# First block of an encoder step: next token rows loaded whole, cached forget logits and constants loaded earlier, query pieces in key tiles

## The chip, the core and the metric

The kernel runs on one core of one Trainium2 chip. The engines of the core work side by side, each through its own queue in order: TensorE (PE; weight loads are shown as PEld), VectorE (DVE), ScalarE (ACT), GpSimd (POOL) and SyncE (SP), which issues most DMAs. An instruction that waits holds up all that stand behind it in its queue. The metric is device time in microseconds; less is better.

## The reference

One inference step of one encoder layer for 2048 prompt tokens and 64 sample tokens with 512 cached positions. Everything is float32.

```python
h = rmsnorm(x, g_pre)
proj = jnp.einsum('bsd,dc->bsc', h, w_in)            # 1024 -> 4104 columns
fq, fk, fv, ff, fg, dq, dk, dv, dg = jnp.split(proj, SPLIT_POINTS, axis=-1)
logf = log_sigmoid(ff + b_f)
cum = jnp.cumsum(logf_all, axis=1)                   # sample: behind the cached logits
fox_o = fox_attention(fq, fk_all, fv_all, cum, ...)  # 8 heads of 64, decay by cum[t] - cum[s]
lam = exp(sum(lq1 * lk1)) - exp(sum(lq2 * lk2)) + lam_init
diff_o = diff_attention(dq1, dq2, dk1, dk2, dv, lam, rel_bias, ...)   # 4 heads
diff_o = rmsnorm(diff_o, subln_g) * (1.0 - lam_init)
mixed = concatenate([fox_o * silu(fg), diff_o * silu(dg)])
y = x + rmsnorm(einsum('bsc,cd->bsd', mixed, w_out), g_post)
```

Returned are y for both token sets and the new rows of fk, fv, logf, dk and dv.

## The kernel before

Each float32 operand of a large product is split into a high and a low part, and a product is three matmuls: high by high, low by high, high by low (L871, L872, L873; for query groups L1026 to L1028). The prompt is cut into four blocks of 512 tokens; the first block carries the 64 sample tokens too. Per block the kernel does the projection in eight column groups of 512: `fv`, `fg`, `fk`, `fq`, `dg`, `dk`, `dq`, `dv`, numbered `gi` 0 to 7 (values, gate, keys and queries of the forgetting attention, `f`, and gate, keys, queries, values of the differential one, `d`). Attention and output projection of earlier blocks run beside the projection of later ones; in the first block there is only the projection, until its attention begins.

A weight group comes in eight row tiles of 128. Each is loaded into a staging tile `wst` (L773; two of them share one buffer of pool `p`, eight buffers), cast on ACT to the high part `wh` (L776), and its rest is made on DVE or POOL as the low part `wl` (L777). The normalised input is kept transposed: `xraw` is loaded (L740), scaled and cast on ACT (`xx`, L744), and DVE makes its low half (L745; L748 for the sample tokens).

The factor 1/rms of each token is applied when a product leaves PSUM (L881 on ACT, into a tile `ef` of four buffers). For the first block the sums of squares come from PE (`ptq`, L1118) and `xv` (L1123, DVE) and end in a root refined by L155 to L158. For the second block they come from the token rows themselves: `stats` loads rows of `xp` as tiles `xn` (L1072) and ACT squares and sums them (L1084). The projection of block 0 emits these squares between the tiles of its groups.

The `wst` loads and their casts run ahead of PE: while PE works on one group, the loads of the next two are issued. In the first block the PSUM tiles of products rotate over five buffers (`acc`); besides, three buffers named `pt` serve `ptq`, the sums of the forget gates and the first tiles of the second group. Values leave through `vhl` (stored to `VS`), gates through `gw` (stored to `GS`), keys are transposed on PE (`ptk`) into `khl` (stored to `KS`), queries are scaled into `qf`, split into `qhl` and stored to `QD`, `QN`. `vhl`, `khl` and some `qhl` share a ring of two buffers, `er`. Attention later loads keys `kg`, queries `qg` and values `vg` from there.

`forget` makes the forget gates; in its step `sample` it loads the cached forget logits (`crev`, L1212), scans them in a row (L1216) and stores the sums (`csum`, L1221). `prologue2` loads the small constants: `subl` (a gain of the differential output), `lamt` (the four lambda vectors, broadcast to all partitions, in an `ef` tile), `relT` and `cbias` (the position bias table and one column of it), and computes `neglam` (two sums on DVE, L1418, an exponential on ACT, L1421) and `cbias` negated (L1428).

All these steps are thunks in one long list, `line`, each with an estimated time; the list is sorted by it and run, and a scheduler then orders the instructions of each engine. `prologue2` has the time 110.0.

## Time and profile before

| what | us |
|---|---|
| runs, median (lowest to highest) | 1772.97 (1772.33 to 1780.28) |
| the profiled execution | 1778.38 |
| its span in the trace | 1776.6 |
| PE busy in the span | 1715.1 |
| DVE, ACT, POOL busy | 1208.8, 1127.0, 761.7 |

The profile gives, for one execution, the busy time of each engine, what ended each idle time, and when each DMA was issued and landed. A row of a timeline reads: start, duration, engine, line and operation, tile written and read, shape, and in brackets the idle time before it and what ended that. `SPq` is SP's queue of DMA issues. PEclk is the clock that PE was granted, 1.00 being full speed.

### The profile page before, as it was taken

How to read it: one execution, taken by the hardware profiler on the slowest of the kernel's cores; microseconds unless marked ns; L12 is line 12 of the kernel's file. 1: busy time of each engine (PE TensorE's matmuls, PEld its weight loads, DVE VectorE, ACT ScalarE, POOL GpSimd, SP SyncE). 2: the span in 40 equal slices, each digit the busy share in tenths (PEclk: the TensorE clock that was granted, in tenths of full speed). 3: DMA queues.
4: the chain of work that ended last, by engine and by line, in shares of the span. 5: the costliest groups of instructions: out<-in, count | busy, mean ns of one | idle time of the engine just before them, and what ended most of it. 6: DMA issues, size and time to landing. Idle time of an engine off the chain costs nothing.

```text
span 1776.6 us, 31312 instructions
## 1 busy us (share of the span) xinstructions
PE 1715.1 (97%) x9844; PEld 1462.7 (82%) x9844; DVE 1208.8 (68%) x3289; ACT 1127.0 (63%) x2518; POOL 761.7 (43%) x1075
## 2 busy tenths in 40 slices
PE   8899999999999999999999999999989999999998
PEld 6697988888787877888888888888878888888887
DVE  5424565566786666766777687877788787767674
ACT  5636465586676765675676567667676656666663
POOL 2313135364444533443324235645685655323341
PEclk9899999999999999999999999999999999999999
DMA  9785688889767667877677666767674455355433
GB/s 249 229 218 185 201 279 284 242 268 278 210 224 242 209 184 222 260 206 243 213 249 212 208 178 196 225 201 224 204 235 155 158 184 180 129 204 166 155 109 111
DMA packets 278981, 369.94 MB, mean 208 GB/s; under 512 B 32080, under 2 KB 167404, under 8 KB 278816
## 3 DMA queue, kind: packets, MB, share of 16 engines
q1 hardware_dynamic: 278000, 365.57, 67.0%
q0 software_dynamic: 672, 2.38, 0.5%
q8 instruction: 78, 1.28, 0.3%
q14 instruction: 87, 0.71, 0.1%
q10 hardware_dynamic: 144, 0.00, 0.0%
HBM read 263.87 MB, written 106.35 MB: 208 GB/s over the span
## 4 chain that ended last, share of the span: by engine, by line
PE 71%; DMA 11%; DVE 6%; ACT 4%; issue 3%; POOL 3%; SPq 1%; DVEq 0%; POOLq 0%; ACTq 0%
PE S L348 11%; PE pt L487 8%; PE acc L871 8%; PE acc L872 7%; PE acc L873 7%; PE av L518 6%; PE avd L518 4%; PE acc L1026 3%; PE acc L1027 3%; PE acc L1028 3%; DMA wraw<-in_w_in 3%; PE acco L1325 2%; PE acco L1327 2%; PE acco L1326 2%; ACT prob L369 2%
## 5 line engine op out<-in xcount | busy, mean ns | idle before, releaser
L369 ACT ACTIVATE prob<-prob,mn 128x1024 f32<-128x1024 f32 (+8 forms) x400 | 356.6, 893 | 152.8 <-DVE mn L356 151.6
L348 PE MATMUL S<-kg,qg 128*128 128x512 f32 (+4 forms) x1344 | 370.7, 371 | 10.9 <-DVE mn L356 6.1
L494 DVE TENSOR_TENSOR ptl<-pt,pth 128x512 fp32r<-128x512 f32 (+3 forms) x456 | 283.6, 637 | 80.1 <-ACT pth L493 77.7
L871 PE MATMUL acc<-wh,xx 128*128 128x512 f32 x752 | 300.6, 403 | 14.3 <-DVE xv L1123 6.2
L872 PE MATMUL acc<-wl,xx 128*128 128x512 f32 x752 | 299.5, 400 | 3.9 <-DVE wl L777 3.9
L873 PE MATMUL acc<-wh,xx 128*128 128x512 f32 x752 | 298.6, 398 | 0.3 <-DVE xx L745 0.2
L493 ACT CAST pth<-pt 128x512 fp32r<-128x512 f32 (+3 forms) x456 | 238.1, 546 | 91.1 <-PE pt L487 78.4
L487 PE MATMUL pt<-ident,prob 128*128 128x128 f32 (+2 forms) x1692 | 256.4, 273 | 7.7 <-DVE prob L596 5.2
L348 PEld LDWEIGHTS S<-kg,qg 128*128 128x128 f32 (+1 forms) x1344 | 225.5, 187 | 46.4 <-DVE mn L356 11.5
L487 PEld LDWEIGHTS pt<-ident,prob 128*128 128x128 f32 (+2 forms) x1692 | 199.3, 141 | 28.1 <-DVE prob L596 6.1
L777 POOL TENSOR_TENSOR wl<-wraw,wh 128x512 fp32r<-128x512 f32 x126 | 169.7, 1363 | 90.9 <-ACT wh L776 85.0
L871 PEld LDWEIGHTS acc<-wh,xx 128*128 128x128 f32 x752 | 143.4, 191 | 43.8 <-issue 6.6
L872 PEld LDWEIGHTS acc<-wl,xx 128*128 128x128 f32 x752 | 143.4, 191 | 30.0 <-DVE wl L777 4.6
L873 PEld LDWEIGHTS acc<-wh,xx 128*128 128x128 f32 x752 | 143.0, 190 | 28.6 <-DVE xx L745 1.2
L518 PE MATMUL av<-pth,vg 128*128 128x256 f32 (+1 forms) x576 | 157.5, 292 | 3.9 <-ACT pth L493 2.3
L405 POOL TENSOR_TENSOR dg<-bias,cmask 128x128 f32<-128x128 f32 (+1 forms) x136 | 65.2, 479 | 208.6 <-DVE mn L356 134.0
L450 POOL TENSOR_SCALAR gate<-gate,rr 128x64 f32<-128x64 f32 (+1 forms) x136 | 64.2, 482 | 182.8 <-DMA gate<-GS 98.9
L518 PE MATMUL av<-ptl,vg 128*64 128x256 f32 (+1 forms) x576 | 138.2, 281 | 1.5 <-DVE ptl L494 1.5
L776 ACT CAST wh<-wraw 128x512 fp32r<-128x512 f32 x168 | 100.6, 621 | 58.3 <-DMA wraw<-in_w_in 44.1
L518 PE MATMUL avd<-pth,vg 128*128 128x256 f32 (+1 forms) x576 | 131.4, 287 | 0.4 <-ACT pth L493 0.4
L356 DVE CUSTOM_DVE_ANT_0 prob<-S,bias,mn 128x512 f32<-128x512 f32 (+4 forms) x200 | 115.4, 577 | 13.6 <-PE S L348 6.6
L518 PEld LDWEIGHTS av<-pth,vg 128*128 128x128 f32 x576 | 109.5, 191 | 14.2 <-ACT pth L493 2.7
(261 smaller groups left out, 3604.6 us busy)
## 6 DMA issues: line engine op xcount, KB each, us to landing
wraw<-in_w_in SPq DMA_DIRECT2D x168, 256.0 KB, 5.2
vg<-VS SPq DMA_DIRECT2D x80, 512.0 KB, 6.3
qg<-QD SPq DMA_DIRECT2D x128, 256.0 KB, 4.4
kg<-KS SPq DMA_DIRECT2D x64, 512.0 KB, 5.1
wst<-in_w_in SPq DMA_DIRECT2D x64, 256.0 KB, 6.3
out<-ef SPq DMA_DIRECT2D x64, 256.0 KB, 2.6
VS<-vhl SPq DMA_DIRECT2D x32, 512.0 KB, 4.8
KS<-khl SPq DMA_DIRECT2D x32, 512.0 KB, 4.4
```

The source lines that it names most:

```text
L348: nc.tensor.matmul(S[:rows, :c1 - c0], q()[s][:, qc:qc + rows], kg()[ki][:, c0 - k0:c1 - k0], start=(s == 0), stop=(s == 1))
L356: nc.vector.tensor_tensor_reduce(out=pr[:rows, a - p0:b - p0], in0=S[:rows, a - c0:b - c0], in1=ap()[:rows, a - b0:b - b0], scale=1.0, sca ...
L369: nc.scalar.activation(out=pr, in_=pr, func=AF.Exp, scale=-1.0, bias=st["m"][:rows, i - 1:i], accum_out=st["s"][:rows, h:h + 1])
L487: nc.tensor.transpose(pt[:rk, off:off + rows], self.key_tile(sts[j], rows, kt, rk), ident[:rows, :rows])
L493: nc.scalar.copy(h[:rk, :off], pt[:rk, :off])
L494: nc.vector.tensor_tensor(out=l[:rk, :off], in0=pt[:rk, :off], in1=r32(h[:rk, :off]), op=ALU.subtract)
L518: nc.tensor.matmul(st["av"][:vs.stop - vs.start, j0 * rows:W], ctxu["v"][kt // 4][:rk, kt % 4, vs], g["p"][part][:rk, o:o + w], start=(kt ...
L776: nc.scalar.copy(h, raw[:, :BLK])
L777: (nc.vector if many or k % 4 == 3 else nc.gpsimd).tensor_tensor(out=l, in0=raw[:, :BLK], in1=r32(h), op=ALU.subtract)
L871: nc.tensor.matmul(a, x[0][:, c0:c0 + rows], wh, start=s, stop=False)
L872: nc.tensor.matmul(a, x[0][:, c0:c0 + rows], wl, start=False, stop=False)
L873: nc.tensor.matmul(a, x[1][:, c0:c0 + rows], wh, start=False, stop=e)
```

## The change

Four edits, all in the projection of the first block and in the constants.

1. The token rows for the second block's statistics are loaded whole, 128 by 1024 in four loads from pool `p`, the weights' ring, instead of eight halves from pool `raw`; one load is ahead of its square instead of two, the second half of the sums `xss` is zeroed, and the squares are emitted with groups 4 and 5 instead of 2 to 5.
2. The cached forget logits are loaded where `forget` allocates its first tile, into a tile of pool `b`; the same tile holds `csum`. Scan and negation thus no longer use two `ef` tiles.
3. The four loads of `prologue2` form a function `loads2` of their own with time 60.0; `lamt` gets a tile of pool `g`. The sums over it and all other arithmetic stay in `prologue2` at 110.0 in the list; the scheduler orders them by when their inputs are asked for.
4. Query pieces of group `fq` that went to the ring `er` go to tiles of the keys' pool `k`.

```diff
@@ -839,7 +839,7 @@
                     for tt in ts:
                         last = tt[-1] == tl[-1]
                         th += self.nat(b, g, tt, w, x, cols, st, last and ends, last and lastg)
-                        if 2 <= gi <= 5:
+                        if (2 if b else 4) <= gi <= 5:
                             th += sq[:1]
                             sq = sq[1:]
                         if b == 0 and gi == 1 and tt[0] == tl[2]:
@@ -1037,6 +1037,7 @@
                     def evac(c=c, i=i, e=e, segs=segs, t0=t0, N=N):
                         f = self.p["e"].tile([P, BLK], F32, name="qf", tag="ef")
                         hl = self.p["raw"].tile([P, BLK], F32R, name="qhl", tag="raw") if nt > BLK and not i else \
+                            self.p["k"].tile([P, 2 * BLK], F32R, name="qhl", tag="k") if nt > BLK and g == "fq" else \
                             self.p["e"].tile([P, 2 * BLK], F32R, name="qhl", tag="er", bufs=2)
                         nc.vector.tensor_tensor(out=f[:, :N], in0=e[i][:, :N], in1=st["rbc"][:, t0:t0 + N],
                                                 op=ALU.mult)
@@ -1060,16 +1061,16 @@
             tl = tilesof[b]
             e = {}
 
-            todo = [(i, t, hf) for i, t in enumerate(tl) for hf in (0, 1)]
-            lead = 2 if b == 1 else 1
+            parts, w = (1, D) if b == 1 else (2, BLK)
+            todo = [(i, t, hf) for i, t in enumerate(tl) for hf in range(parts)]
+            lead = 1
 
             def load(n):
                 i, t, hf = todo[n]
-                e[n] = self.p["raw"].tile([P, BLK], F32, name="xn", tag="raw") if b == 1 else \
+                e[n] = self.p["p"].tile([P, 2 * BLK], F32, name="xn", tag="p") if b == 1 else \
                     self.p["e"].tile([P, BLK], F32, name="xn", tag="ef")
-                nc.sync.dma_start(out=e[n], in_=xp[t * P:(t + 1) * P, hf * BLK:(hf + 1) * BLK])
+                nc.sync.dma_start(out=e[n], in_=xp[t * P:(t + 1) * P, hf * w:(hf + 1) * w])
 
             def square(n):
                 def go():
@@ -1077,6 +1078,8 @@
                     if not n:
                         e["ss"] = sm.tile([P, 2, 8], F32, name="xss", tag="xss", bufs=2)
                         nc.vector.memset(e["ss"], 1.0)
+                        if parts == 1:
+                            nc.vector.memset(e["ss"][:, 1, :], 0.0)
                         for m in range(lead):
                             load(m)
                     if n + lead < len(todo):
@@ -1134,6 +1137,10 @@
 
             def alloc():
                 e["z"] = self.p["raw"].tile([P, BLK + DEC], F32, name="z8", tag="z", bufs=1)
+                if b == 0:
+                    t = self.p["b"].tile([P, BW], F32, name="crev", tag="b")
+                    e["rev"], e["csum"] = t[:8, :BLK], t[:8, BLK:]
+                    nc.sync.dma_start(out=e["rev"], in_=clf)
             th.append((0.0, alloc))
             for c0, N in ((0, BLK), (BLK, DEC))[:1 + (b == 0)]:
                 def step(c0=c0, N=N):
@@ -1206,10 +1213,8 @@
                 nc.sync.dma_start(out=lf_s, in_=z[:DEC, 32:40])
                 pt = ps.tile([P, BLK], F32, name="pts", tag="pt", bufs=3)
                 nc.tensor.transpose(pt[:8, :DEC], z[:DEC, 32:40], ident[:DEC, :DEC])
-                c = self.p["e"].tile([P, BLK], F32, name="csum", tag="ef")[:8]
+                c, r = e["csum"], e["rev"]
                 c2 = sm.tile([8, DEC], F32, name="csn", tag="csn", bufs=1)
-                r = self.p["e"].tile([P, BLK], F32, name="crev", tag="ef")[:8]
-                nc.sync.dma_start(out=r, in_=clf)
                 nc.vector.tensor_tensor_scan(out=c2, data0=ones[:8].to_broadcast([8, DEC]), data1=pt[:8, :DEC],
                                              initial=0.0, op0=ALU.mult, op1=ALU.add)
                 nc.sync.dma_start(out=CS[:, PAST:], in_=c2)
@@ -1408,23 +1413,29 @@
         nc.vector.tensor_tensor(out=wf[:, :, 32:40], in0=wv, in1=r32(wf[:, :, 0:8]), op=ALU.subtract)
         nc.sync.dma_start(out=fb, in_=bass.AP(fbias.tensor, fbias.offset, [[0, P], [1, 8]]))
 
+    held = {}
+    def loads2(g):
+        nc.sync.dma_start(out=subl, in_=subln)
+        held["lam"] = g.tile([P, 2, P], F32, name="lamt", tag="g").rearrange("p a c -> p (a c)")
+        nc.sync.dma_start(out=held["lam"], in_=bcast_row(lams, 256))
+        held["rt"] = sm.tile([4, 32], F32, name="relT", tag="relT", bufs=1)
+        nc.sync.dma_start(out=held["rt"], in_=relT)
+        nc.sync.dma_start(out=cbias, in_=bass.AP(relT.tensor, relT.offset + 15, [[0, P], [32, 4]]))
     def prologue2(e):
-        nc.sync.dma_start(out=subl, in_=subln)
-        lam = e.tile([P, BLK], F32, name="lamt", tag="ef")
-        nc.sync.dma_start(out=lam[:, :256], in_=bcast_row(lams, 256))
+        lam, rt = held["lam"], held["rt"]
         ee = sm.tile([P, 4], F32, name="lame", tag="lame", bufs=1)
         for i in (0, 1):
-            nc.vector.tensor_tensor_reduce(out=lam[:, 256:320], in0=lam[:, 128 * i:128 * i + 64],
+            nc.vector.tensor_tensor_reduce(out=lam[:, 128 * i:128 * i + 64], in0=lam[:, 128 * i:128 * i + 64],
                                            in1=lam[:, 128 * i + 64:128 * i + 128], scale=1.0, scalar=0.0,
                                            op0=ALU.mult, op1=ALU.add, accum_out=ee[:, i:i + 1])
         nc.scalar.activation(out=ee[:, 2:4], in_=ee[:, 0:2], func=AF.Exp)
         nc.vector.tensor_tensor(out=neglam, in0=ee[:, 3:4], in1=ee[:, 2:3], op=ALU.subtract)
         nc.vector.tensor_scalar(out=neglam, in0=neglam, scalar1=LAM_INIT, scalar2=None, op0=ALU.subtract)
 
-        rt = sm.tile([4, 32], F32, name="relT", tag="relT", bufs=1)
-        nc.sync.dma_start(out=rt, in_=relT)
-        nc.sync.dma_start(out=cbias, in_=bass.AP(relT.tensor, relT.offset + 15, [[0, P], [32, 4]]))
         nc.vector.tensor_scalar(out=cbias, in0=cbias, scalar1=-1.0, scalar2=None, op0=ALU.mult)
         ln = e.tile([P, BLK], F32, name="line", tag="ef")[:4]
         ln2 = e.tile([P, BLK], F32, name="line2", tag="ef")[:4]
@@ -1472,6 +1483,7 @@
         put(lst, t, t + cost(lst))
         if b == 0:
             line.append((20.0, len(line), lambda: prologue(pe)))
+            line.append((60.0, len(line), lambda: loads2(pools["g"])))
             line.append((110.0, len(line), lambda: prologue2(pe)))
             for h in range(4):
                 line.append((150.0 + 25.0 * h, len(line), lambda h=h: prologue3(h)))
```

The lines of the changed kernel are shifted by up to 12 from the place of each edit on. Where the constants are loaded, SP's queue held before, from the last `xraw` of the first block on (`xn` are the token rows, `subl`, `relT` and `cbias` the constants):

```order
L740 DMA xraw<-in_xT 128x576
L773 DMA wst<-in_w_in 128x512 x8
L1072 DMA xn<-in_xp 128x512 x5
L773 DMA wst<-in_w_in 128x512 x2
L1412 DMA subl<-in_subln 128x1
L1426 DMA relT<-in_relT 4x32
L773 DMA wst<-in_w_in 128x512 x2
L1427 DMA cbias<-in_relT 128x4x1
L773 DMA wst<-in_w_in 128x512 x2
L1072 DMA xn<-in_xp 128x512 x2
L773 DMA wst<-in_w_in 128x512 x2
```

The same place on SP in the changed kernel (`crev` are the cached logits, `CS` the store of their sums):

```order
L740 DMA xraw<-in_xT 128x576
L1143 DMA crev<-in_clf 8x512
L773 DMA wst<-in_w_in 128x512 x8
L1420 DMA subl<-in_subln 128x1
L1422 DMA lamt<-in_lams 128x256
L1424 DMA relT<-in_relT 4x32
L1425 DMA cbias<-in_relT 128x4x1
L773 DMA wst<-in_w_in 128x512 x4
L1226 DMA CS<-crev 8x512
L773 DMA wst<-in_w_in 128x512 x4
```

Seven loads of token rows are gone from here; the load of `crev` stands ahead of the eight weight tiles and the four constants stand right behind them, `lamt` among them. The eight are those of group `fk`, the pieces behind them those of `fq`.

On DVE, from the end of the first group's low halves to the root that the first evacuations need, stood before:

```order
L745 SCALAR_TENSOR_TENSOR xx<-xraw,gcol,xx 128x576
L748 SCALAR_TENSOR_TENSOR xx<-xraw,gcol,xx 128x64
L777 TENSOR_TENSOR wl<-wst,wh 128x512 x4
L1123 TENSOR_SCALAR xv<-ptq 128x4
L1123 TENSOR_SCALAR xv<-ptq 64x1
L155 TENSOR_TENSOR rt_463<-xrs 128x8
L156 TENSOR_TENSOR rt_464<-rt_463,xv 128x8
L1428 TENSOR_SCALAR cbias<-cbias 128x4
L157 TENSOR_SCALAR rt_464<-rt_464 128x8
L158 TENSOR_TENSOR xrs<-xrs,rt_464 128x8
```

and now, up to `xv` (behind which the root follows without a row between; ISA rows are the two sums over `lamt`):

```order
L1221 SCALAR_TENSOR_TENSOR crev<-ones,crev 8x512
L745 SCALAR_TENSOR_TENSOR xx<-xraw,gcol,xx 128x576
L748 SCALAR_TENSOR_TENSOR xx<-xraw,gcol,xx 128x64
L1224 TENSOR_SCALAR crev<-crev 8x511
L777 TENSOR_TENSOR wl<-wst,wh 128x512 x2
L1432 ISA lamt,lame<-lamt 128x64
L1432 ISA lame 128x1
L1432 ISA lamt,lame<-lamt 128x64
L1432 ISA lame 128x1
L1439 TENSOR_SCALAR cbias<-cbias 128x4
L1436 TENSOR_TENSOR neglam<-lame 128x1
L1437 TENSOR_SCALAR neglam<-neglam 128x1
L777 TENSOR_TENSOR wl<-wst,wh 128x512 x2
L1126 TENSOR_SCALAR xv<-ptq 128x4
```

The scan of the cached logits moved ahead of the last low half of the input; `lamt`'s sums, `cbias` and `neglam` moved ahead of the last two low weights and of `xv`. At the scan's old place DVE went from the gates straight to `crev` and then to the eight low weights of group `fk`:

```order
L1000 SCALAR_TENSOR_TENSOR gw<-ef,gw 128x512
L1216 SCALAR_TENSOR_TENSOR crev<-ones,crev 8x512
L1218 MEMSET csum 8x1
L1219 TENSOR_SCALAR csum<-crev 8x511
L777 TENSOR_TENSOR wl<-wst,wh 128x512 x8
```

where now the three rows between are gone. The token rows stand further back on SP, at the key stores (`KS`), with the query stores (`QD`) behind:

```order
L970 DMA out<-ef 128x512
L1073 DMA xn<-in_xp 128x1024
L989 DMA KS<-khl 128x8x128
L1073 DMA xn<-in_xp 128x1024 x3
L773 DMA wst<-in_w_in 128x512 x2
L989 DMA KS<-khl 128x8x128
L970 DMA out<-ef 64x512
L773 DMA wst<-in_w_in 128x512 x3
L1052 DMA QD_94<-qhl 128x256
L1053 DMA QD_94<-qhl 128x512
```

Before, the eight `wst` loads of group `dk` stood here in one piece; now four loads of token rows go ahead of it, it comes in pieces of 2, 3 and 3, and the last three stand among the query stores.

## The prediction

> **What bounds the kernel now.** I read the page first: TensorE (PE) works nearly all the time, so a change that adds no matmul can gain only where PE waits or runs at a lowered clock.
> ```profile
> span 1776.6 us, 31312 instructions
> PE 1715.1 (97%) x9844; PEld 1462.7 (82%) x9844; DVE 1208.8 (68%) x3289; ACT 1127.0 (63%) x2518; POOL 761.7 (43%) x1075
> PE   8899999999999999999999999999989999999998
> ```
> The slices with idle time are the first four of 44 us each, which hold the first block's projection, and the change's new order lies there too: behind about 160 us PE, ACT and VectorE (DVE) meet the same instructions in the same order, and time saved ahead of that point reaches the end whole. So the next view is busy time and granted clock of PE in those stretches, cut at its long waits.
> ```profile
> core 0: us, PE busy (x), PEclk, DMA share, GB/s
> 0.00:39.30 39.30, 36.26 (x170) 1.00 0.90 234
> 39.30:45.40 6.10, 0.00 (x0) 0.89 0.97 319
> 45.40:51.00 5.60, 5.57 (x13) 0.51 0.78 258
> 51.00:76.70 25.70, 25.05 (x114) 1.00 0.69 233
> 76.70:80.50 3.80, 0.00 (x0) 1.00 0.50 167
> 80.50:86.00 5.50, 5.46 (x17) 0.69 0.75 263
> 86.00:129.00 43.00, 43.00 (x262) 1.00 0.91 210
> 129.00:139.00 10.00, 6.79 (x50) 1.00 0.82 258
> 139.00:170.00 31.00, 31.00 (x130) 0.94 0.63 200
> ```
> Three stalls, and behind each PE runs for a while at a lowered clock: 5.60 us at 0.51 hold 5.60 × 0.49 = 2.7 us of lost time, 5.50 at 0.69 hold 1.7, and 31 at 0.94 hold 1.9. PE's waits from 0 to 170 us name who released each:
> ```profile
> PE acc L871 <- DVE xv L1123: 6.2, 1, 6.2
> PE acc L872 <- DVE wl L777: 3.9, 1, 3.9
> PE acc L871 <- ACT wh L776: 3.7, 2, 3.2
> PE ptf L1195 <- DVE fz L1187: 0.6, 1, 0.6
> ```
> Columns: total us, times, longest. All that the change can win is 6.2 + 2.7, 3.9 + 1.7, 3.2 + 1.9 and 0.6: some 20 us of 1778.4, the profiled execution's own time.
>
> **The first stall (39.3 to 45.4 us).** The group that follows the first needs PSUM buffers that `ptq` shares, and L1123 reads `ptq` behind the last low weights (L777) on DVE. Those wait for ScalarE (ACT), which waits for the next token rows:
> ```profile
> 40.24 0.63 ACT L1084 ACTIVATE xn<-xn 128x512 f32<-128x512 f32 x1 [7.72 <-DMA xn<-in_xp]
> 44.47 0.69 DVE L777 TENSOR_TENSOR wl<-wst,wh 128x512 fp32r<-128x512 f32 x1 [2.28 <-ACT wh L776]
> 45.08 0.21 DVE L1123 TENSOR_SCALAR xv<-ptq 128x4 f32<-128x4 f32 x2
> ```
> The change takes the squares and their loads out of this place. But in DVE's queue two sums over `lamt`, the negation of `cbias` and two instructions for `neglam` now stand ahead of the last two low weights, and so ahead of `xv`. What is late next is the landing of these constants. They are issued behind eight weight tiles:
> ```profile
> 23.05 6.72 SPq L773 DMA_DIRECT2D wst<-in_w_in  x8
> SPq L1412 <- DMA wst<-in_w_in: 1.2, 1, 1.2
> 39.54 0.33 SPq L1412 DMA_DIRECT2D subl<-in_subln  x1
> 42.26 6.64 DMA cbias<-in_relT
> 48.92 0.17 DVE L1428 TENSOR_SCALAR cbias<-cbias 128x4 f32<-128x4 f32 x1 [2.75 <-DMA cbias<-in_relT]
> ```
> Before, the load at 39.54 us waited 1.2 us for a weight tile, the last of those eight (it is the eighth DMA ahead of `subl`): so these weights have landed only by about 39.5 us, 10 us behind their issue. `cbias` is 2 KB and yet took 6.64 us. If the constants keep their place behind the weights, `cbias` is there between 41 us (39.5 and a short transfer) and 45 us (39.5 + most of 6.64). Behind it DVE still does 0.17 for `cbias`, 0.24 + 0.15 for `neglam`, two low weights at 0.69 and `xv` at 0.21, about 2.2 us. PE starts again between 43.2 and 47.2 us, against 45.4: a gain of 2.2 to a loss of 1.8, and the half clock stays. The value nearest the row is the middle: **0**.
>
> The Trainium skill, page "DMA: Bandwidth & Descriptors", section "Queues, rings and completion order", says that each DMA engine consumes the descriptors of a queue in ring order. That speaks against this edit, since a small load cannot pass 2 MB queued ahead of it; the 6.64 us for 2 KB agree. By the rule this term is 0 or a loss, without it a gain of up to the 8.9 us of the stall and its clock.
>
> **The wait for `fz` (0.6 us).** In the row above, DVE stood 2.75 us for `cbias` in the middle of the root that all evacuations of the first group need. In the new order nothing stands there, so the forget gates come earlier against PE: **+0.6**.
>
> **The second stall (76.7 to 80.5 us).**
> ```profile
> 78.22 1.21 DVE L1216 TENSOR_TENSOR_SCAN crev<-ones,crev 8x512 f32<-8x512 f32 x1 [7.13 <-DMA crev<-in_clf]
> 79.81 4.89 DVE L777 TENSOR_TENSOR wl<-wst,wh 128x512 fp32r<-128x512 f32 x8
> 78.85 0.69 ACT L881 ACTIVATE ef<-acc,xrs 128x512 f32<-128x512 f32 x1 [5.08 <-DMA GS<-ef]
> ```
> DVE waits 7.13 us for the cached forget logits, then scans them, and only then makes the low weights that PE waits for. Loaded ahead of the eight weights at 23.05 us, and scanned there, they are out of DVE's queue here: the low weights follow their casts at once. ACT's wait is another: an evacuation needs an `ef` buffer that a gate store still reads. The two `ef` buffers of the scan are now free, so that evacuation waits for an older store. What I expect is that the stall and its clock go: **+3.9 + 1.7 = 5.6**; should ACT's wait hold the last five casts behind it as now, all but 1 us of it stays (rival C).
>
> The scan itself moves ahead of the last low half of the input:
> ```profile
> 29.01 0.82 DVE L745 SCALAR_TENSOR_TENSOR xx<-xraw,gcol,xx 128x576 fp32r<-128x576 f32 x1 [0.66 <-ACT xx L744]
> 30.50 0.39 PE L871 MATMUL acc<-wh,xx 128*128 128x512 f32 x1
> ```
> With 1.21 us it ends that half near 31.0 instead of 29.8, about when PE wants it. Up to 1 us of delay there lies in front of the first stall, whose end is set by the constants: **0**, and 1 us if that cover is gone.
>
> **The third stall (129 to 139 us).**
> ```profile
> 124.42 0.55 ACT L1049 CAST qhl<-qf 128x256 fp32r<-128x256 f32 x2 [7.55 <-DMA KS<-khl]
> 131.86 1.61 SPq L1415 DMA_DIRECT2D lamt<-in_lams  x1
> 136.28 0.22 DVE L1418 CUSTOM_DVE_ANT_0 lamt<-lamt 128x64 f32<-128x64 f32 x1 [6.91 <-DMA lamt<-in_lams]
> 136.81 0.20 ACT L1421 ACTIVATE lame<-lame 128x2 f32<-128x2 f32 x1 [7.90 <-DVE lame L1418]
> 137.71 0.61 ACT L776 CAST wh<-wst 128x512 fp32r<-128x512 f32 x1
> L348 PE MATMUL S<-kg,qg x54: 220/332/477, 188.4 to 297.3; 128*128 128x128 f32 x14, 128*128 128x256 f32 x14, 128*128 128x384 f32 x14, 128*128 128x512 f32 x12
> ```
> The load of `lamt` is late because it needs an `ef` buffer; DVE and ACT stand 7 to 8 us for it, and the casts that PE waits for stand behind. Both go with the early load; and query pieces that waited 7.55 us for key stores (the shared `er` ring) get `k` buffers. The first key loads of the attention, which owned these, now stand behind the last query stores on SP; the scores (L348, the last row) first read keys at 188.4 us, some 40 us on, which hides it. **+3.2 + 1.9 = 5.1**.
>
> **The moved token rows.** They are 2 MB, as before, now in four loads among the key stores, ahead of the weights of the differential keys, whose last tiles wait until squares have freed the ring; PE asks for those only after the whole gate group, so that they have time.
> ```profile
> 29.82 6.69 SPq L1072 DMA_DIRECT2D xn<-in_xp  x5
> xn<-in_xp SPq DMA_DIRECT2D x7, 256.0 KB, 8.2
> ```
> Before, a 256 KB load landed in 8.2 us; a 512 KB one takes from 8 to 16. On ACT each square is twice 0.63 us at most, four are 5.0. Behind them ACT holds the fox query casts, which PE needs only when its PSUM is full: the first block has five buffers, and a tile of 24 matmuls lasts 24 × 43.00/262 = 3.9 us by the stretch from 86 to 129 us, which gives some 16 us of cover. So **0**, with up to 5 us lost if a load lands later than that cover.
>
> **Sum.** 0 + 0.6 + 5.6 + 0 + 5.1 + 0 = 11.3 us at full price. In no row is the second wait of ACT shown to vanish; I leave 1 us of it. 10.3 us off the profiled 1778.4 make 1768.1; the profiled execution stood 5.4 us above the runs' median of 1772.97, so against the median it is **1762.7 us**.
>
> **Rivals.**
> *A, the forecast*: 0.50; own range 1760 to 1766 (the first term from +2.2 to −1.8, the remainder of the second stall 0 to 2).
> *B, the constants land early.* If the small loads are not held behind the weights, `xv` comes with the last weight at about 40 us; 3 us or less of the first stall is left, and some or all of the 2.7 us of clock goes too: another 3 to 6 us, 1757 to 1760. For it: PE's wait is named to DVE and ACT, not to a DMA. Against: 6.64 us for 2 KB. 0.17. How much of the clock returns, the rows leave open: waits of 3.9 and 3.2 us cost 1.7 and 1.9 us behind them. The Trainium skill, page "TensorE: Matmul & The Clock Gate", section "Part 1: The HAM clock gate (the "warmup" mystery)", has the clock halved after an idle window of about 3.4 us; by that a rest of 3 us would mostly cost none, by the rows in proportion 1.5.
> *C, the second stall stays in part.* ACT's evacuation of the gate group still waits for a gate store that queues behind other transfers: at most 1 of its 5.08 us goes, DVE's low weights then wait for ACT, and PE waits 3 instead of 3.9 us with its clock lowered. The sum is 0.6 + 1 + 5.1, about 6: 1767. 0.20.
> *D, the moved squares keep the third stall.* If a token row lands late, ACT stands at its square, the query casts come behind, and behind these the casts of the gate group, for which PE stopped at 138 us. A delay of 3 us keeps that stall with its clock, 5 us of what is won: 1768 to 1770. 0.08.
> *E, slower.* The moved token rows fill the PSUM cover: squares stand on ACT behind loads that land over 16 us after the first square's turn, query casts stand behind them, and PE stops. It decides from four loads taking more than 16 us together; at a landing of 16 us each, one behind the other from the third on, PE loses 14 us and its clock 2 more, against 11 won: 1778, up to 1784. Nothing in the stretch from 86 to 129 us (DMA 0.91 busy, 210 GB/s) excludes it; that 2 MB at 210 GB/s are 10 us speaks against. 0.05.
>
> **From cases to numbers.** The range 1757 to 1770 holds A, C, nearly all of D and the greater part of B. Half a percent (8.9 us, about what a measurement of this kernel can tell from no change) puts the border of faster at 1764.1, inside A: two thirds of A and all of B give 0.33 + 0.17, a little of C 0.03, faster 0.53; the rest of A, C, D and part of E make 0.44 the same; the upper part of E slower, 0.03.
>
> **What would show it.** PE's first stall ends with `xv` behind `cbias` on DVE, at 43 to 47 us, at half clock after it: A; at 41 us, B. In PE's waits no wait over 1 us for L777 near 77 us, and none for L776 near 138 us; ACT's wait for a gate store under 2 us: otherwise C. No wait of PE for `acc` PSUM near 110 to 125 us: otherwise D or E. The prediction is wrong if DVE stands longer than to 45 us for a constant, or if the gain ahead of 160 us is lost again behind it, where I assume the same order means the same pace.

## The result and the profile after

In 20 runs each, the changed kernel has a median of 1765.95 us (1760.43 to 1773.49) against 1776.81 us (1772.33 to 1783.70) before: a ratio of 0.9938, 95% interval 0.9928 to 0.9949, or 11 us of gain with 9 to 13 as its interval. The prediction had 10.3 us. Its 1762.7 us was counted from the median of three runs before, 1772.97 us, which 20 runs put at 1776.81; so the gain agrees and the time itself lies 3.2 us above. The profiled execution of the changed kernel took 1771.98 us, 6 us above its median, so the spans of the two profiles differ by only 6.4 us.

From the page of the changed kernel, the span, the engines' busy times and PE's slices; then PE's busy time and granted clock, cut at its waits, and the waits themselves from 30 to 200 us:

```profile
span 1770.2 us, 31297 instructions
PE 1712.9 (97%) x9844; PEld 1458.2 (82%) x9844; DVE 1203.0 (68%) x3290; ACT 1125.3 (64%) x2510; POOL 762.7 (43%) x1075
PE   8999999999999999999999999999989999999998
```

```profile
core 0: us, PE busy (x), PEclk, DMA share, GB/s
0.00:41.90 41.90, 37.92 (x170) 0.96 0.89 230
41.90:44.10 2.20, 0.05 (x2) 1.00 0.97 344
44.10:50.00 5.90, 5.85 (x19) 0.71 0.83 281
50.00:69.00 19.00, 19.00 (x90) 1.00 0.76 261
69.00:75.00 6.00, 6.00 (x28) 1.00 0.66 168
...
151.80:155.00 3.20, 0.01 (x1) 1.00 0.41 159
155.00:170.00 15.00, 14.94 (x58) 0.89 0.12 41
```

```profile
PE acc L871 <- ACT wh L776: 3.3, 1, 3.3
PE acc L871 <- DVE xv L1126: 2.2, 1, 2.2
PE ptq L1121 <- POOL xsq L755: 0.7, 1, 0.7
```

The second stall and the third are gone with their lowered clock; the matmuls that stood behind them now start without a wait, at 73.5 and 126.2 us. The first is shorter, and a **new one of 3.2 us** stands at 151.8 us, where the kernel before had none.

To see what each stretch brought, the same matmul is looked up in both traces: both programs have 9844, and the n-th starts earlier in the changed kernel by its *lead*. I take it at four places, named by the time that the kernel before needs: behind the first stall (58.9 us), the second (96.4), the third (147.8) and at 211.6 us, from where PE, ACT and DVE have the same order. One execution has a lead at each place; the first two rows, two executions of the same program, show how much that varies. Each ratio is to runs of the kernel before that were made beside it.

| run | 58.9 | 96.4 | 147.8 | 211.6 | median us | ratio to before (95%) |
|---|---|---|---|---|---|---|
| the change | 2.3 | 8.8 | 14.1 | 7.8 | 1765.95 | 0.9938 (0.9928 to 0.9949) |
| the change, again | 6.4 | 12.6 | 17.9 | 14.0 | 1767.42 | 0.9931 (0.9910 to 0.9953) |
| rows back | 0.3 | 6.8 | 12.1 | 9.9 | 1765.49 | 0.9935 (0.9911 to 0.9959) |
| logits back | 3.2 | 9.7 | 15.0 | 12.4 | 1763.31 | 0.9922 (0.9902 to 0.9941) |
| constants back | 5.5 | 12.0 | 15.6 | 13.3 | 1763.29 | 0.9921 (0.9902 to 0.9941) |
| er ring back | 2.5 | 9.1 | 14.3 | 14.1 | 1763.78 | 0.9920 (0.9901 to 0.9940) |
| er ring, late arithmetic | 7.2 | 8.5 | 13.7 | 13.4 | 1764.15 | 0.9916 (0.9893 to 0.9939) |
| rows alone | 3.9 | 6.7 | 11.9 | 11.9 | 1764.07 | 0.9914 (0.9894 to 0.9934) |
| logits alone | 0.8 | 7.3 | 4.7 | 3.8 | 1775.43 | 0.9977 (0.9963 to 0.9991) |
| constants alone | 0.0 | 2.5 | 7.8 | 3.1 | 1770.03 | 0.9953 (0.9937 to 0.9969) |
| key tiles alone | 0.3 | 0.4 | 3.5 | 1.6 | 1778.28 | 0.9992 (0.9981 to 1.0004) |
| rows and logits | 5.0 | 11.6 | 16.8 | 15.8 | 1762.42 | 0.9905 (0.9885 to 0.9925) |

Behind 212 us the leads of single profiles still drift with the order unchanged: at the end, 1550 us later, they stand between 6.6 us lower and 8.4 us higher; the medians, not one lead at the end, say what a kernel is worth.

**The first stall** in the changed kernel, DVE's timeline:

```profile
39.10 0.23 DVE L1432 CUSTOM_DVE_ANT_0 lamt<-lamt 128x64 f32<-128x64 f32 x1 [5.67 <-DMA lamt<-in_lams]
42.20 0.17 DVE L1439 TENSOR_SCALAR cbias<-cbias 128x4 f32<-128x4 f32 x1 [2.73 <-DMA cbias<-in_relT]
```

DVE stands 5.67 us for `lamt` and 2.73 us for `cbias`; `xv` is made behind them and PE starts again at 44.15 us. The wait is 4.0 us shorter than before, and yet PE starts only 1.3 us earlier (44.15 against 45.44), because it gets there later, at 41.95 instead of 39.27 us. A wait for `xsq` ahead of `ptq` and a stretch at half clock behind it cost most of that; PE's timeline, and a window of PE:

```profile
34.75 1.26 PE L1121 MATMUL ptq<-ones,xsq 128*128 128x1 f32 x10 [0.69 <-POOL xsq L755]
37.30:40.70 3.40, 3.40 (x9) 0.50 0.74 207
```

The prediction put nothing for either. The wait for `xsq` stands, with 0.5 to 0.7 us, in all six profiles that have both the rows and the logits moved, and with 0.3 us or less in the others; its cause was not sought.

In the second profile of the same kernel DVE has the constants some 3 us earlier, and PE waits 0.5 us:

```profile
38.91 0.22 DVE L1432 CUSTOM_DVE_ANT_0 lamt<-lamt 128x64 f32<-128x64 f32 x1 [4.49 <-DMA lamt<-in_lams]
39.35 0.17 DVE L1439 TENSOR_SCALAR cbias<-cbias 128x4 f32<-128x4 f32 x1
```

```profile
PE acc L871 <- DVE xv L1126: 0.5, 1, 0.5
```

**The new stall** in the changed kernel: from the timelines of PE, ACT and POOL, then SP's waits from 130 to 150 us, then SP's timeline:

```profile
155.06 0.73 PE L871 MATMUL acc<-wh,xx 128*128 128x512 f32 x2 [3.25 <-ACT wh L776]
153.21 0.63 ACT L997 ACTIVATE gw<-ef 128x512 f32<-128x512 f32 x1 [8.34 <-DMA GS<-ef]
144.36 1.29 POOL L1002 TENSOR_TENSOR ef<-ef,gw 128x512 f32<-128x512 f32 x1 [3.80 <-DMA QN<-qhl]
```

```profile
SPq L194 <- DMA QD<-qhl: 4.3, 1, 4.3
SPq L194 <- DMA QN<-qhl: 3.4, 1, 3.4
SPq L1053 <- DMA wst<-in_w_in: 3.4, 2, 1.7
SPq L773 <- DMA wst<-in_w_in: 1.5, 1, 1.5
```

```profile
149.10 0.53 SPq L194 DMA_DIRECT2D kg<-KS  x1
149.72 16.44 SPq L1004 DMA_DIRECT2D GS<-ef  x4
```

Read upwards: the key loads (L194) get their tiles only when the query pieces in them are stored, so they stand on SP for 4.3 and 3.4 us. Two gates were ready at 140.6 and 145.7 us (L1002 starts at 139.28 and 144.36 and takes 1.29), but their stores stand behind the last key load and go out from 149.72. They hold `ef` buffers meanwhile; ACT waits 8.34 us for one, the casts of the next group wait behind ACT, and PE waits for those. The key loads are not all of the delay: between the last two of them, two query stores (L1053) and a weight load (L773) wait 4.9 us more for weights to land. (The program's DMAs on SP use eight semaphores in turn, so that none goes out before the eighth ahead of it has landed.)

### The profile page after: what moved, and what is told of

It reads as the page before. It is cut to its first block, busy times and chain, and to the rows that moved or that the text cites. A ratio compares the mean times of both kernels' runs of the same rounds, so it can differ in the third digit from the quotient of the medians.

```text
span 1770.2 us, 31297 instructions
## 1 busy us (share of the span) xinstructions
PE 1712.9 (97%) x9844; PEld 1458.2 (82%) x9844; DVE 1203.0 (68%) x3290; ACT 1125.3 (64%) x2510; POOL 762.7 (43%) x1075
## 5 line engine op out<-in xcount | busy, mean ns | idle before, releaser
L348 PEld LDWEIGHTS S<-kg,qg 128*128 128x128 f32 (+1 forms) x1344 | 224.8, 187 | 48.0 <-DVE mn L356 13.7
L356 DVE CUSTOM_DVE_ANT_0 prob<-S,bias,mn 128x512 f32<-128x512 f32 (+4 forms) x200 | 115.3, 577 | 13.3 <-PE S L348 5.3
```

The lines of the kernel that those rows point to most:

```text
L348: nc.tensor.matmul(S[:rows, :c1 - c0], q()[s][:, qc:qc + rows], kg()[ki][:, c0 - k0:c1 - k0], start=(s == 0), stop=(s == 1))
L356: nc.vector.tensor_tensor_reduce(out=pr[:rows, a - p0:b - p0], in0=S[:rows, a - c0:b - c0], in1=ap()[:rows, a - b0:b - b0], scale=1.0, sca ...
```

## The experiments

### Each edit undone

The fences of this part hold the lines that tell the edits apart; the rest of each edit is left out.

```diff
# rows back                    (edit 1: halves from pool raw, lead 2)
-                        if (2 if b else 4) <= gi <= 5:
+                        if 2 <= gi <= 5:
-            parts, w = (1, D) if b == 1 else (2, BLK)
+            todo = [(i, t, hf) for i, t in enumerate(tl) for hf in (0, 1)]
# logits back                  (edit 2: in sample)
-                c, r = e["csum"], e["rev"]
+                c = self.p["e"].tile([P, BLK], F32, name="csum", tag="ef")[:8]
+                r = self.p["e"].tile([P, BLK], F32, name="crev", tag="ef")[:8]
+                nc.sync.dma_start(out=r, in_=clf)
# constants back               (edit 3)
-            line.append((60.0, len(line), lambda: loads2(pools["g"])))
+        lam = e.tile([P, BLK], F32, name="lamt", tag="ef")     # in prologue2, with its loads
# er ring back                 (edit 4)
-                            self.p["k"].tile([P, 2 * BLK], F32R, name="qhl", tag="k") if nt > BLK and g == "fq" else \
```

*Rows back*, expected:

> Only edit 1 undone: token rows again as eight halves, squared during the first groups. Theory: what the rows cost in the first block is the first stall alone; ACT's squares stand again ahead of the last casts, and the constants land later behind five more loads, so xv comes at 46 to 50 us instead of 43.8 and 2 to 6 us of the gain of 11 are lost; PE's wait for wh of 3.3 us near 152 us stays, since it hangs on the key loads. Rival: the wait near 152 us comes from the moved rows, which push the next weights back; then it is gone here and the time about that of the change.

Half right: PE restarts at 46.10 us after 4.4 us for `xv`, and nothing is gained on the first stall (lead 0.3). `cbias` is used at 41.26 us, between the 42.20 and 39.35 of the change; what holds `xv` is the last low weight, which waits for a cast that stands on ACT behind four squares:

```profile
45.14 0.69 DVE L777 TENSOR_TENSOR wl<-wst,wh 128x512 fp32r<-128x512 f32 x1 [2.81 <-ACT wh L776]
```

No time is lost in the runs (0.9935 against 0.9938). The new stall takes 2.2 us of lead here and does not go, so it does not need the moved rows; that it was 5.4 and 2.8 us in the change leaves open whether they make it longer.

*Logits back*, expected:

> Only edit 2 undone: cached logits loaded in the sample step into ef tiles. Theory: DVE waits for crev again ahead of the low weights of fk, PE stands 3 to 4.5 us near 71 to 75 us with its clock lowered behind it; about 5.7 us lost, some 5 of the 11 us left. Rival: the stall had been ACT's, waiting for a gate store, and DVE's wait only lay beside it; then it comes back with under 1.5 us, because the constants no longer take ef tiles.

Wrong. DVE scans the logits where it did before, and PE does not stop: the second stretch still brings 6.5 us. SP's timeline of the kernel before, then SP's and DVE's of this run:

```profile
70.91 0.74 SPq L1212 DMA_DIRECT2D crev<-in_clf  x1
```

```profile
66.14 0.29 SPq L1215 DMA_DIRECT2D crev<-in_clf  x1
```

```profile
69.25 1.21 DVE L1219 TENSOR_TENSOR_SCAN crev<-ones,crev 8x512 f32<-8x512 f32 x1 [0.25 <-issue]
71.70 1.29 DVE L777 TENSOR_TENSOR wl<-wst,wh 128x512 fp32r<-128x512 f32 x2 [0.78 <-ACT wh L776]
```

The load goes out at 66.14 instead of 70.91 us and its scan starts 3.1 us later instead of 7.3 (78.22 - 70.91), so that it is over before the first cast is done. Of the 9.0 us by which the scan is earlier, 4.8 come from the issue: ahead of it SP stores `fz`, for which it stood 3.6 us in the kernel before and 0.4 here. The other 4.2 come from a shorter time between issue and scan, for which the runs give no cause. SP's waits of the kernel before, from 55 to 76 us:

```profile
SPq L1188 <- DVE fz L1187: 3.6, 1, 3.6
```

*Constants back*, expected:

> Only edit 3 undone: constants loaded in prologue2, lamt in an ef tile. Theory: lamt comes late again, DVE and ACT stand for it near 122 to 128 us, PE waits 2 to 4 us for wh and runs at a lowered clock behind; the first stall is shorter by 1 to 2 us, since nothing stands ahead of xv; in sum 2 to 4 us lost. Rival: the third stall came from query pieces in the er ring, which stay in key tiles here; then no wait near 125 us, and the time is 1 to 2 us better than the change.

Right in part. PE restarts at 42.58 us and the first stretch brings 5.5 instead of 2.3 us (but 6.4 in the second profile of the change). `lamt` is late again, DVE stands 4.2 us for it, and the third stretch brings 3.6 instead of 5.3; but PE waits only 1.3 us there, for a low weight, and its clock stays at 1.00. No 2 to 4 us are lost. That nothing stands ahead of `xv` was wrong, since DVE stands 5.20 us for `cbias` in front of it:

```profile
40.93 0.17 DVE L1433 TENSOR_SCALAR cbias<-cbias 128x4 f32<-128x4 f32 x1 [5.20 <-DMA cbias<-in_relT]
```

*The er ring back*, expected:

> Only edit 4 undone: fq pieces in the er ring again. Theory: the key loads no longer wait on SP for query stores to land, the gate stores go out as they are made, and PE's wait for wh of 3.3 us near 152 us with its lowered clock is gone, 5 us; the third stall stays away or comes back with at most 1.5 us, since lamt is early: 3 to 5 us better than the change, a ratio to before of about 0.991. Rival: the er ring made the third stall; then PE waits 3 us or more near 120 to 130 us, and the time is that of the change or worse by up to 2 us.

Right in the profile: the new stall is gone, the third does not come back, and the lead of 14.3 us at 147.8 is still 14.1 at 211.6. SP issues the last key load at 125.97 and the gate stores from 143.95 us, 3.6 us behind the first gate instead of 9.1; ACT waits for a gate store 3.3 instead of 8.34 us, and PE's waits from 30 to 200 us hold none for `wh`:

```profile
PE acc L871 <- DVE xv L1125: 3.9, 1, 3.9
PE ptq L1120 <- POOL xsq L755: 0.6, 1, 0.6
```

In time it stands at 0.9920 against 0.9938 of the change, with intervals that overlap; and the second profile of the change has a lead of 14.0 us at 211.6 as well.

So no edit is needed for the gain as a whole. The second and the third stall stay away whichever edit is undone, but for a rest of 1.3 us without the constants; only the first comes back, without the rows. The next runs ask which edit suffices.

### Each edit alone, on the kernel before

```diff
# rows alone
-                        if 2 <= gi <= 5:
+                        if (2 if b else 4) <= gi <= 5:
+            parts, w = (1, D) if b == 1 else (2, BLK)
# logits alone
+                    t = self.p["b"].tile([P, BW], F32, name="crev", tag="b")
+                    nc.sync.dma_start(out=e["rev"], in_=clf)
# constants alone
+            line.append((60.0, len(line), lambda: loads2(pools["g"])))
# key tiles alone
+                            self.p["k"].tile([P, 2 * BLK], F32R, name="qhl", tag="k") if nt > BLK and g == "fq" else \
```

*Rows alone*, expected:

> The kernel before with edit 1 alone. Theory (the stalls have several causes, and the rows are one of most): PE restarts near 42.5 us, the forget gates come some 3 us earlier relative to PE, crev is loaded earlier and the second stall falls under 1.5 us though crev is where it was; the third stall stays at about 3 us, since lamt and the er ring are as before. Lead at 212 us 9 to 12 us, ratio about 0.994. Rival (each edit has its own stall, as predicted): 2 to 3 us from the first stall, the second stays at 3.5 us or more; lead 2 to 4 us, ratio 0.998.

The time is that of the whole change (0.9914 against 0.9938, intervals overlapping): **the rows alone bring the gain**, though the other three bring it without them too (rows back, 0.9935). PE restarts some 3 us earlier (3.9 us of lead). This is the edit that the first stall hangs on: in all eight profiles with the rows moved PE restarts between 40.8 and 44.2 us, in all five without between 45.4 and 46.1. At the second stall SP and DVE show what follows from that:

```profile
65.80 0.29 SPq L1213 DMA_DIRECT2D crev<-in_clf  x1
```

```profile
69.07 1.21 DVE L1217 TENSOR_TENSOR_SCAN crev<-ones,crev 8x512 f32<-8x512 f32 x1 [0.66 <-issue]
73.17 1.29 DVE L777 TENSOR_TENSOR wl<-wst,wh 128x512 fp32r<-128x512 f32 x2 [2.44 <-ACT wh L776]
```

DVE waits for ACT there, no longer for the logits; 2.8 us are won, and a wait of 1.8 us for `wh` is left, above the 1.5 expected. The third stall goes whole (5.2 us), which I had not expected. `lamt` is still late, but the scheduler now puts the casts that PE waits for ahead of the exponential on ACT. ACT's queue as the programs have it, before and with the rows alone:

```text
before                                rows alone
L1421 ACTIVATE lame<-lame 128x2       L776 CAST wh<-wst 128x512
L1049 CAST qhl<-qf 128x256            L1049 CAST qhl<-qf 128x256
L1049 CAST qhl<-qf 128x64             L776 CAST wh<-wst 128x512 x7
L776 CAST wh<-wst 128x512             L1049 CAST qhl<-qf 128x256
L1049 CAST qhl<-qf 128x256            L1049 CAST qhl<-qf 128x64
L776 CAST wh<-wst 128x512 x7          L1422 ACTIVATE lame<-lame 128x2
```

ACT's timeline of the run with the rows alone agrees: the casts run at 126.92 us, the exponential 8 us later, and no cast or matmul waits for it.

```profile
126.92 3.74 ACT L776 CAST wh<-wst 128x512 fp32r<-128x512 f32 x7
131.47 0.55 ACT L1049 CAST qhl<-qf 128x256 fp32r<-128x256 f32 x2 [0.80 <-DMA QN<-qhl]
135.44 0.20 ACT L1422 ACTIVATE lame<-lame 128x2 f32<-128x2 f32 x1 [3.42 <-DVE lame L1419]
```

*Logits alone*, expected:

> The kernel before with edit 2 alone. Both theories: the first stall stays (about 6 us), the second goes, the third stays. By the theory of several causes lead at 212 us 4.5 to 6 us, ratio about 0.997; rival: ACT's wait for a gate store keeps the second stall at 2 us or more, lead under 3 us.

The second stall goes (6.5 us), as both theories had it, but at the third PE waits longer than before (4.8 instead of 3.2 us): PE came earlier, and `lamt`, with the exponential ahead of the casts, no earlier by as much. A good part of the won time is waited away at the next place, and 3.8 us are left.

*Constants alone*, expected:

> The kernel before with edit 3 alone. Theory: xv stands behind the constants and the token rows, so the first stall is as long as before or up to 4 us longer; the second stall stays or is shorter, since lamt asks for no ef tile; the third goes (under 1 us), as in the run where only the er ring was back. Lead at 212 us 0 to 5 us. Rival: the third stall needs both edits 3 and 4; then about 3 us of it stay and the lead is 0 or negative.

The first stretch brings nothing, the second 2.5 us, the third stall goes (5.3 us), and 3.8 us are lost again right behind it. Of PE's two longest waits from 60 to 215 us the first stands at the second stall (77.6 us); the other is new, at 142.0 us with 3.4 us of half clock behind it, and makes up most of that loss:

```profile
PE acc L871 <- ACT ef L881: 1.7, 1, 1.7
PE acc L871 <- ACT wh L776: 1.4, 1, 1.4
```

At 211.6 us 3.1 us are left, while the runs say 8.4 us (5.5 to 11.2); the rest came behind that place, within the drift that other profiles show there, and I have no cause for it. By the runs alone this edit cannot be told from the whole change either (0.9953 against 0.9938, intervals overlapping).

*Key tiles alone*, expected:

> The kernel before with edit 4 alone. Theory: first and second stall as before; the third is shorter by up to 4 us, since only lamt is late; then the key loads wait on SP for query stores and the wait for wh near 160 us comes up with 1 to 3 us: lead at 212 us -2 to 3 us, no measurable difference. Rival: the er ring made the third stall alone; then it goes and the lead is 4 to 5 us.

As expected in lead and time: 3.1 us won at the third stall, 1.9 lost behind it, with ACT standing 5.30 us for a gate store, and no difference in time (0.9992). The expected wait for `wh` behind it did not come; PE waits 0.6 us for a low weight there, at 167.4 us.

### Two further versions

The late arithmetic takes the `er` ring and moves the arithmetic on the constants behind the first root; their loads stay early.

```diff
-        ee = sm.tile([P, 4], F32, name="lame", tag="lame", bufs=1)
+        ee = sm.tile([P, 40], F32, name="lame", tag="fd", bufs=1)
+        nc.vector.memset(ee[:, 4:5], -1.0)
-        nc.vector.tensor_scalar(out=cbias, in0=cbias, scalar1=-1.0, scalar2=None, op0=ALU.mult)
+        nc.vector.tensor_scalar(out=cbias, in0=cbias, scalar1=ee[:, 4:5], scalar2=None, op0=ALU.mult)
```

> The change with fq pieces in the er ring, and with the arithmetic on the constants (the two sums, the exponential, neglam, the negation of cbias) tied to the buffer of the forget gates' fd, so that it comes behind the first root instead of ahead of xv; the loads stay early. Theory: in the first stall xv stood behind the landing of cbias alone, so PE waits under 1 us for xv, starts the second group at 41 to 42.5 us at an unlowered clock, and nothing comes back later; PE leads the kernel before by 17 to 20 us at 212 us (the run with the er ring led by 14). Rival: xv stands behind the weights' casts and landing as well; then PE still waits 2 to 4 us there and the lead stays at 14 to 15.

The first stall is gone: DVE makes `xv` at 36.98 us, 7 us earlier than in the change, and the lead is 7.2 us. That shows what held it. But the time is given back at once:

```profile
48.72 0.58 ACT L878 COPY ef<-accS 64x512 f32<-64x512 f32 x1 [5.86 <-DMA out<-ef]
```

```profile
PE ptf L1201 <- DVE lame L1430: 3.7, 1, 3.7
```

Evacuations begin earlier, fill the four `ef` buffers, and ACT stands 5.86 us for their stores; the forget gates, which come behind, are no earlier, and PE waits 3.7 us for them (the profile names DVE's next instruction, `lame`, but `fz` ends just ahead of it). With 13.4 us at 211.6, where 17 to 20 were expected, it is no better than with the er ring alone; the rival's wait for `xv` did not come either.

Rows and logits, without the constants and the key tiles:

> Edits 1 and 2 without 3 and 4. Theory from the runs so far: the rows alone take away most of the first and the third stall, the logits what is left of the second; without the constants ahead of xv PE restarts near 42.6 us and leads by some 12 us at 96 us, without key tiles for query pieces there is no wait near 152 us, and the third stall stays away as with the rows alone: lead at 212 us 16 to 18 us, the highest of all, ratio 0.990 or less. Rival: with PE earlier, lamt in its ef tile and the er ring make the third stall again, 3 to 5 us; lead 12 to 14 us.

Right within 0.2 us of lead: 15.8 us at 211.6, the highest of all, and the lowest median, 1762.42 us. All of PE's waits from 30 to 200 us:

```profile
PE ptq L1120 <- POOL xsq L755: 0.7, 1, 0.7
PE av L518 <- ACT pth L493: 0.3, 1, 0.3
PE acc L1026 <- ACT wh L776: 0.2, 1, 0.2
```

There is no wait for `xv` any more; but behind the wait for `xsq` PE runs at half clock from 38.1 us for 3.4 us, and gets to the second group only at 42.97 us. It beats the kernel before beyond doubt (0.9905). That it beats the change (0.9931 in the same set of runs) is not shown: the intervals overlap, and its lead of 15.8 us is one execution, where the change has 7.8 and 14.0 in two.

The change itself beside these two sets:

> The change itself once more, beside the others on one chip. Theory: PE waits 2 to 4 us for xv near 43 us, over 2.5 us for wh near 152 us with ACT waiting there for a gate store, lead at 212 us 7 to 10 us; the gain in time 9 to 13 us. If the wait near 152 us was a draw of one execution, it is under 1 us here and the lead 13 to 14 us.

The wait near 152 us is there again, smaller: ACT stands 6.4 us for a gate store, and the lead falls from 17.9 to 15.0. Over all runs with the query pieces in key tiles, six profiles, the stretch from 147.8 to 181 us (by the kernel before) costs 5.4, 2.8, 2.2, 2.6, 2.2 and 1.7 us; in the four with the rows moved and the er ring it costs 0.0 to 0.4.

## Why the prediction was right, and where not

- **What bounds the kernel**: right. What could be traced of the gain lies in PE's stalls of the first 200 us and the clock behind them; behind 212 us single profiles drift too much to tell.
- **First stall, 0 (from +2.2 to −1.8)**: the mechanism was right as far as `xv` behind `cbias`, and in the recorded profile PE restarts at 44.15 us, inside the forecast 43.2 to 47.2. That the weights ahead of it on SP are what makes `cbias` late was not tried: no run loads it ahead of them. The term was too small: 1.3 us from the earlier start and 1.0 from a clock less lowered behind it make 2.3, and 6.4 in the second profile, where PE restarts near 41.6 us. The early constants of rival B are what that second execution of the same program shows. A gain in both profiles also goes against the "0 or a loss" that the prediction drew from the ring order here. The prediction took PE's arrival at this stall as given; it came 2.7 us later, with the wait for `xsq` and the half clock.
- **`fz`, +0.6**: right; the wait is gone, and the lead rises from 2.3 to 3.1 us there.
- **Second stall, +5.6, of which I left 1 us**: right in size (5.75), nothing of it stays, and rival C fell. (Rival C's own terms make 6.7 us and 1766, not about 6 and 1767.) The reason given is one that suffices, as the logits alone show, and not one that is needed: with the logits at their old place and the rows moved the stall is gone as well, their load going out 5 us earlier.
- **Third stall, +5.1**: right in size (5.3). Of the two reasons given the early `lamt` suffices by itself (5.3), the key tiles remove 3.1 us and leave a wait of 1.7; the rows alone remove it too (5.2), with another order of ACT's queue.
- **Moved rows, 0**: right at their new place. The squares end at 110 us and PE waits for nothing there, so rivals D and E did not come. Squares stood 1.9 us for their loads in all; the one load whose landing the trace holds took 5.9 us, where the working had 8 to 16. What was missed is the other side of this edit: the rows' absence suffices for the gain.
- **The step that failed**: "first read keys at 188.4 us, some 40 us on, which hides it". I had named the reader of the key loads, and not what stands behind them in SP's queue: gate stores, whose `ef` buffers ACT needs, with the casts behind. It cost 5.4 us in the recorded profile and 2.8 in the other, and with it came one of the signs that the prediction had named for being wrong: a gain lost again, here 14.1 us of lead down to 7.8.
- **The sum, 10.3 us**: measured 11.0 (9.1 to 12.8). That it came out so near is partly luck, since two errors go against each other: the first stall brought 2 to 6 us more, the new stall took 3 to 5.

That, with the rows moved, the first stall is not held by ACT's casts or the weights is shown by the late arithmetic, in one profile. That the key tiles cause the new stall is shown by the er ring, where it is gone; that they do so through the key loads is read from the order of SP's queue and its waits; a version with key tiles but other places for the key loads was not tried. Why ACT's queue has the exponential behind the casts once the rows are moved is the scheduler's doing and was only read off, not tried by itself.

## What to carry to other kernels

Terms that are read from separate stalls do not add up by edit: take each edit out and put each in alone before crediting it, since here one of four sufficed, the other three did without it, and one of them cost what it won. When a load is made to wait for a buffer, ask not only who reads it, but what stands behind it in the queue that issues it. A stall removed early is worth only what the next late thing leaves: logits alone won 6.5 us and kept 3.8. Nor is the shortening of a wait the gain: ask when the engine now gets there.

## What the runs showed of the hardware

The same small load of the same program was used by DVE at 42.20 us in one profile and at 39.35 us in another, with the same instructions ahead of it, and a stall of 2.2 us was one of 0.5.

A stall costs more than itself. Behind waits of 2.2 and 3.25 us PE's granted clock was 0.71 for 5.9 us and 0.89 for 15 us, 1.7 us each. Behind the shorter waits of the second profile, 0.5 and 1.3 us, it stayed full; PE's windows there:

```profile
41.80:50.00 8.20, 8.20 (x39) 1.00 0.94 336
...
146.00:160.00 14.00, 12.09 (x50) 1.00 0.15 58
```

The Trainium skill, page "TensorE: Matmul & The Clock Gate", section "Part 1: The HAM clock gate (the "warmup" mystery)", has the clock halved after an idle window of about 3.4 us. The waits of 0.5 and 1.3 us agree; the wait of 2.2 us is shorter than that window and yet stands ahead of a lowered clock. So does the wait of 0.7 us for `xsq`, in both profiles of the change, while behind the same 0.7 us with the constants back the clock stayed full; windows of the second profile of the change and of the constants back:

```profile
36.50:39.90 3.40, 3.40 (x9) 0.50 0.92 228
35.20:42.00 6.80, 5.61 (x42) 1.00 0.91 254
```

From 20 to 215 us, in all 13 traces, each lowered piece holds the clock at 0.50 for 3.4 or 6.8 us, whatever the wait ahead of it; 0.71 over 5.9 us and 0.89 over 15 are one such piece of 3.4 us each. What makes a piece begin these runs do not tell.
